# Scheduler ranks for small-tile products, and a reversed operand order in their groups, in a bidirectional RWKV-7 and gated-MLP trunk

## The chip, the cores and the metric

The kernel is one program on one core of a Trainium2 chip. The metric is device time in microseconds (us) of one execution; several executions are made and the median is given. The engines that matter here are PE (TensorE, the matmuls), DVE (VectorE), ACT (ScalarE) and POOL (GpSimd). Each engine works through its own queue of instructions in order and waits on semaphores where an operand comes from another engine or from a DMA.

## The reference

Two residual layers and a final norm over x of 1 x 256 x 2048. Layer 0 is a bidirectional RWKV-7 mixer: one wide projection, token shift, then for 64 heads of width 64 a state recurrence in both directions. Layer 1 is a gated MLP whose spatial mixing takes 128 positions at a time. All that the change touches belongs to layer 0:

```python
def wkv_scan(r, w, k, v, a, b, reverse):
    # S_t = S_(t-1) diag(w_t) + (S_(t-1) a_t) b_t^T + v_t k_t^T ;  y_t = S_t r_t
    ...

def rwkv7_bidir_mixer(h, w_in, mu_prev, mu_next, ...):
    z = h @ w_in
    zs, gate = z[..., :SHIFT_COLS], z[..., SHIFT_COLS:]
    zs = zs + mu_prev * (shift_prev(zs) - zs) + mu_next * (shift_next(zs) - zs)
    r, k, v, dw, da = jnp.split(zs, ...)
    ...
    for d, rev in ((0, False), (1, True)):
        wll = -jax.nn.softplus(-(w0[d] + jnp.tanh(dw[:, :, d]) @ w_up[d])) - 0.5
        decay = jnp.exp(-jnp.exp(wll))
        a_d = jax.nn.sigmoid(a0[d] + da[:, :, d] @ a_up[d])
        k_d = k * (1.0 + (a_d - 1.0) * k_a)
        y = y + wkv_scan(rh, heads(decay), heads(k_d), vh, -kk, kk * heads(a_d), rev)
        bonus = bonus + jnp.sum(rh * heads(k_d) * r_k, axis=-1, keepdims=True) * vh
    yn = (group_norm(y) * ln_w + ln_b)
    return ((yn + bonus) * jax.nn.silu(gate)) @ w_out
```

## The kernel before

Layer 0 is cut into 16 blocks (NB) of 256 of the 4096 branch columns, four heads each. In one block two tiles of 128 columns (`cl` or `l`) hold two heads each, and the two heads of a tile lie in the two halves of the 128 partitions: `h` = 0 is the lower half, `h` = 1 the upper (`H[h]`). The 256 tokens are cut into four chunks of 64 (`c`, or `i` in the recurrence), and there are two directions `d`. The recurrence is done chunk by chunk in matrix form, so a block consists of large products and of many small ones:

- **Full products** are the projections. `mains` computes k, r, v and g of a block (PSUM tiles `acck`, `accr`, `accv`, `accg`). Weights come by DMA as f32 and are split into a high part (`whi`, ACT, L150) and a low part (`wlo`, DVE, L151); `mm3` (L165, L166, L167) then makes three products for each tile of weights: high weights with the high part of the activations, high with low, low with high. Each is 128x128 weights on 128x256 data, and one of k, r, v, g of a block takes 96 of them. `rates` makes the low-rank decay products `up` in the same way.
- **gp** (`grams`, L584): for one direction and one `cl`, four chunks times two halves, eight products. Each contracts over 64 partitions, that is over one half of PE's rows: h=0 the lower half, h=1 the upper. There is one PSUM tile for each half. Both have the tag `pg`, which has two buffers; DVE multiplies each with the mask into `Gs` (L589) and so frees it. `bp` (L606) and other transposed factors use `pg`, too.
- **qp** (`inverses`, L651 and L657): 32x32 products of the triangular inverse. DVE solves the 32x32 diagonal blocks in a loop (L637 to L639) and transposes them (`TD`, L642; `Tn`, L643); L651 takes `Tn`.
- **The recurrence** (`chain`): for each chunk i, eight products of 64 columns in each group. xp (L714, takes the state SUV), yp with RC (L717), then `Xs` copied by ACT, uu (L723), copied back into SUV by ACT (L725), then sp (L730) and yp (L732), DVE makes the next state, and ACT copies it into SUV (L742). Here h picks a half of PE's columns (the output rows); the contraction is over all rows.
- **vp** (L674, transposes of v), **bb** (L769) and **yt** (`finish`, L777, transposes of the normed output, 16 of them) close a block.

The parts of a block are generators that yield a due time within a period; a loop at the end of the layer always advances the one with the smallest due time, and this sets the order of the program text: in one pass it interleaves the projections of block p with grams and inverses of block p-1 and the recurrence of block p-2. This order is not the order of the engines. The kernel is built with

```python
    with _tile.TileContext(nc, schedule_with_timeline_sim=True) as tc:
```

which means that the framework simulates the engines' time lines while it builds and gives each engine, step by step, an instruction whose operands it expects to be ready; among the ready ones it takes the one that stands first in the program text. So small products are placed among the full ones at build time, one by one; a group of eight can be cut.

What the change touches: the loops that issue gp, qp, xp, yp, uu, sp and yt, and the generator `each` that gives the order of (d, l, h) in the recurrence's groups.

Of the kernel before, what the change touches and what calls it, by code (L numbers as in the profile page):

```python
# [22 lines left out]
def trunk(tc, x, norm_g, final_norm_g, w_in, mu_prev, mu_next, w0, w_up, a0, a_up, k_k, k_a, r_k,  # L23
          ln_w, ln_b, w_out, g_w_in, g_ln_g, g_ln_b, g_w_s, g_b_s, g_w_out, out):
    nc = tc.nc
    V, S, G, PE = nc.vector, nc.scalar, nc.gpsimd, nc.tensor
# [9 lines left out]
    C = 64  # L36
    NC = T // C
# [392 lines left out]

    MT = PERIOD / 16
    dt = 4 * MT / KT

# [136 lines left out]
    def grams(b, f, d):  # L572

        AR, BK = f["AR"], f["BK"]
        if d == 0:
            f["Gs"] = sc.tile([P, 2, 16, 2 * C], F32, tag="Gs", name=f"Gs{b}", bufs=2)
        Gs = f["Gs"]
        for cl in range(2):
            yield TGP[d][cl]

            gp = [sm(f"gp{b}_{h}{d}{cl}").rearrange("p (c q t) -> p c q t", c=NC, q=2) for h in range(2)]
            for c in range(NC):
                for h in range(2):
                    PE.matmul(gp[h][:, c].rearrange("p q t -> p (q t)"),  # L584
                              BK[H[h], d, cl, c].rearrange("p q t -> p (q t)"),
                              AR[H[h], d, cl, c].rearrange("p q t -> p (q t)"), start=True, stop=True)
            u0 = (d * 2 + cl) * NC
            for h in range(2):
                V.tensor_tensor(Gs[:, h, u0:u0 + NC], gp[h].rearrange("p c q t -> p c (q t)"),  # L589
                                gmask[:, d].rearrange("p q t -> p (q t)").unsqueeze(1).to_broadcast([P, NC, 2 * C]),  # L590
                                ALU.mult)
# [19 lines left out]
    def inverses(b, f):  # L611

        Gs, AR = f["Gs"], f["AR"]

        def lane(name):
            return se.tile([P, 16 * 33], F32, tag="ln", name=f"{name}{b}", bufs=3)

        Dt = lane("Dt")[:, :512].rearrange("p (t u) -> p t u", u=16)
        NQ = sc.tile([P, 16, 32], F32, tag="vy", name=f"NQ{b}", bufs=2)
        for h in range(2):  # L620
            for q in range(2):
                r0 = h * 64 + q * 32
                S.copy(Dt[r0:r0 + 32].rearrange("p t u -> p u t"), Gs[q * 32:q * 32 + 32, h, :, q * 32:q * 32 + 32])
            nc.sync.dma_start(NQ[h * 64:h * 64 + 32], Gs[0:32, h, :, 32:64])
        yield TSUB[0]
        La = se.tile([P, 32, 32], F32, tag="La", name=f"La{b}")
        V.transpose(La, Dt.unsqueeze(2).to_broadcast([P, 32, 2, 16]))
        xs = lane("X")
        G.memset(xs[:, :512], 0.0)
        G.tensor_scalar(xs.rearrange("p (m r) -> p m r", r=33)[:, :, 0:32:16], diag, 1.0, None, ALU.mult)  # L630
        X = xs[:, :512].rearrange("p (s t) -> p s t", t=16)
        TD = lane("TD")[:, :512]
        for j in range(31, 0, -1):
            yield TSUB[1] - (TSUB[1] - TSUB[0] - 2) * j / 31
            m, n = j // 2, 16 - j // 2
            tv = TD[:, :j * n].rearrange("p (s t) -> p s t", t=n)
            V.tensor_tensor(tv, La[:, j, 0:j].unsqueeze(2).to_broadcast([P, j, n]),  # L637
                            X[:, j:j + 1, m:].to_broadcast([P, j, n]), ALU.mult)
            V.tensor_tensor(X[:, 0:j, m:], X[:, 0:j, m:], tv, ALU.add)  # L639
        yield TSUB[1]  # L640
        Tn = lane("Tn")[:, :512]
        V.transpose(TD.rearrange("p (u t h) -> p t h u", t=16, h=2), X.rearrange("p s t -> p t s"))  # L642
        V.transpose(Tn, TD)  # L643
        TD, Tn = [t.rearrange("p (u t) -> p u t", t=32) for t in (TD, Tn)]
        qp = sm(f"qp{b}", "pq", 1).rearrange("p (u t) -> p u t", t=32)
        R0 = [slice(h * 64, h * 64 + 32) for h in range(2)]
        R1 = [slice(h * 64 + 32, h * 64 + 64) for h in range(2)]
        yield TQ[0]
        for u in range(16):
            for h in range(2):  # L650
                PE.matmul(qp[R1[h], u], NQ[R0[h], u], Tn[R0[h], u], start=True, stop=True)  # L651
        for h in range(2):
            S.copy(NQ[R1[h]], qp[R1[h]])
        yield TQ[1]
        for u in range(16):
            for h in range(2):
                PE.matmul(qp[R0[h], u], NQ[R1[h], u], TD[R1[h], u], start=True, stop=True)  # L657
# [30 lines left out]
    def chain(b, f):  # L688
# [6 lines left out]
        def part(name, i):  # L695
            return sm(f"{name}{b}_{i}", "pc", 1)[:, :256].rearrange("p (n v) -> p n v", v=C)

        def each(i):

            for d, l in DL:  # L700
                for h in range(2):
                    yield d, l, h, (d * 2 + l) * NC + i, SUV[:, d, l, i, h]

        def y(d, l, h, i):
            return yp[H[h], l if d == 0 else 1 - l, i if d == 0 else NC - 1 - i]

        SJ = None
        for i in range(NC):
            t = TCH + CT * i
            yield t  # L710

            xp = part("xp", i)
            for d, l, h, u, suv in each(i):
                PE.matmul(xp[H[h], d * 2 + l], Gs[:, h, u, 0:C], suv, start=True, stop=True)  # L714
            if i > 0:
                for d, l, h, u, suv in each(i):
                    PE.matmul(y(d, l, h, i), RC[:, h, u], suv, start=False, stop=False, skip_group_check=True)  # L717
            Xs = sc.tile([P, 4, C], F32, tag="Xs", name=f"Xs{b}_{i}")
            S.copy(Xs, xp)
            yield t + CB[0]  # L720
            up = part("uu", i)
            for d, l, h, u, _ in each(i):
                PE.matmul(up[H[h], d * 2 + l], TTs[:, h, u], Xs[:, d * 2 + l], start=True, stop=True)  # L723
            for h in range(2):
                S.copy(SUV[H[0], :, :, i, h].rearrange("p d l v -> p (d l) v"), up[H[h]])  # L725
            yield t + CB[1]
            if i < NC - 1:
                sp = part("sp", i)
                for d, l, h, u, suv in each(i):
                    PE.matmul(sp[H[h], d * 2 + l], BT[:, h, u], suv, start=True, stop=True)  # L730
            for d, l, h, u, suv in each(i):
                PE.matmul(y(d, l, h, i), Gs[:, h, u, C:2 * C], suv, start=False, stop=False, skip_group_check=True)  # L732
# [13 lines left out]
    def finish(b, f):  # L746
# [24 lines left out]
        V.tensor_tensor(OT, bb, Vt, ALU.mult)  # L771
        yield TYT
        yt = sm(f"yt{b}", "pc", 1).rearrange("p (l t) -> p l t", l=2)
        for cl in range(2):
            for c in range(NC):
                for h in range(2):
                    PE.matmul(yt[H[h], cl, c * C:(c + 1) * C], yn[:, cl * NC + c], ident[:, H[h]],  # L777
                              start=True, stop=True)
        SG = f["SG"]
        for cl in range(2):  # L780
            j = 2 * b + cl
# [390 lines left out]
```

## Time and profile before

| | before |
|---|---|
| median of 3 runs | 2211.72 us (2210.79 to 2213.2) |
| the profiled execution, whole | 2209.93 us |
| the profiled execution, span | 2208.1 us |
| mean granted TensorE clock | 0.994 |
| layer 0's blocks in the span | about 40 to 1420 us, some 78 us a block |

How to read the rows. "busy" is the time in which an engine worked, x the count of instructions. A timeline row gives start, duration, engine, line, operation, output <- inputs by the program's names (block numbers left out), tile shape, and how many neighbouring records it joins; an f32 product is two records, so x16 is a group of eight products. A matmul's duration is longer than the distance to the next, since PE pipelines them; costs are therefore taken between starts. A row of waits gives the waiting engine, tile and line, what released it, the time, how often, and the longest. In the table of windows, behind the window and its length, stand the busy times of PE, PEld (weight loads), DVE, ACT and POOL with counts, then the granted clock, the DMA share and GB/s. A window of 156 us is two blocks.

### The profile page before, as it was taken

What the parts mean: (1) busy time and instruction counts of PE and PEld (TensorE: products, weight loads), DVE (VectorE), ACT (ScalarE), POOL (GpSimd) and SP (SyncE); (2) the same over time, 40 slices, a digit from 0 to 9 for tenths busy, and PEclk for the clock granted to TensorE, in tenths of its full rate; (3) what the DMA queues carried; (4) which work ended last, traced back from release to release, by engine and by line L of the source; (5) the groups of instructions that cost most, each with busy time, mean ns of one, the idle gap of its engine ahead of it and who ended that gap; (6) DMA issues with size and microseconds to landing.
All of it is one profiled execution on the core that took longest, in us unless ns stands there. A gap on an engine that the chain in (4) does not pass through costs nothing.

```text
span 2208.1 us, 48735 instructions
## 1 busy us (share of the span) xinstructions
PE 2169.0 (98%) x19984; PEld 1938.5 (88%) x19984; DVE 1611.7 (73%) x3121; ACT 1289.0 (58%) x2032; POOL 160.7 (7%) x230
## 2 busy tenths in 40 slices
PE   7999999999999999999999999999999999999998
PEld 7899999999999999999999877788888888888886
DVE  5788788888887988897888764475456777777444
ACT  6556666757666766766676654464444444444443
POOL 2210110111101100010011000000000000000000
PEclk9899999999999999999999999999999999999999
DMA  5556455454555555555555565676766666666664
GB/s 167 141 144 158 116 130 135 131 138 128 139 134 146 140 137 137 143 139 139 145 140 135 167 193 179 195 248 191 229 200 191 193 196 193 195 197 191 196 195 153
DMA packets 403374, 362.30 MB, mean 164 GB/s; under 512 B 128848, under 2 KB 350800, under 8 KB 403024
## 3 DMA queue, kind: packets, MB, share of 16 engines
q1 hardware_dynamic: 382896, 337.96, 53.9%
q10 hardware_dynamic: 20256, 21.24, 3.0%
q8 instruction: 157, 2.57, 0.5%
q14 instruction: 65, 0.53, 0.1%
HBM read 329.78 MB, written 6.29 MB: 152 GB/s over the span
## 4 chain that ended last, share of the span: by engine, by line
PE 77%; DMA 8%; DVE 7%; ACT 6%; issue 2%; POOL 0%; SPq 0%; ACTq 0%; POOLq 0%; DVEq 0%
PE uacc L204 5%; PE gacc L204 5%; DMA raw_o<-in_rwkv_w_out_dram 3%; PE gp L584 3%; PE oacc L166 3%; PE oacc L167 3%; PE oacc L165 3%; PE uacc L206 3%; PE gacc L206 3%; PE vacc L165 3%; PE vacc L166 3%; PE vacc L167 3%; PE accg L167 2%; PE accv L167 2%; PE accv L165 2%; PE accv L166 2%
## 5 line engine op out<-in xcount | busy, mean ns | idle before, releaser
L204 PE MATMUL uacc<-z,whi_u 128*128 128x512 f32 x512 | 179.0, 394 | 0.0
L204 PE MATMUL gacc<-z,whi_g 128*128 128x512 f32 x512 | 177.3, 393 | 0.0
L165 PE MATMUL acck<-zh,whi_wk 128*128 128x256 f32 x512 | 151.1, 295 | 1.6 <-ACT whi_wk L150 1.6
L167 PE MATMUL accg<-zh,wlo_wg 128*128 128x256 f32 x512 | 149.2, 291 | 3.1 <-DVE wlo_wg L151 2.8
L165 PE MATMUL accg<-zh,whi_wg 128*128 128x256 f32 x512 | 151.9, 297 | 0.0
L167 PE MATMUL accr<-zh,wlo_wr 128*128 128x256 f32 x512 | 149.3, 292 | 0.1
L165 PE MATMUL accv<-zh,whi_wv 128*128 128x256 f32 x512 | 148.9, 291 | 0.0
L165 PE MATMUL accr<-zh,whi_wr 128*128 128x256 f32 x512 | 148.9, 291 | 0.0
L166 PE MATMUL accr<-zl,whi_wr 128*128 128x256 f32 x512 | 148.8, 291 | 0.0
L167 PE MATMUL accv<-zh,wlo_wv 128*128 128x256 f32 x512 | 148.4, 290 | 0.1
L167 PE MATMUL acck<-zh,wlo_wk 128*128 128x256 f32 x512 | 146.1, 285 | 1.0 <-DVE wlo_wk L151 1.0
L166 PE MATMUL accv<-zl,whi_wv 128*128 128x256 f32 x512 | 146.7, 287 | 0.0
L166 PE MATMUL acck<-zl,whi_wk 128*128 128x256 f32 x512 | 146.0, 285 | 0.0
L166 PE MATMUL accg<-zl,whi_wg 128*128 128x256 f32 x512 | 145.7, 285 | 0.0
L206 PE MATMUL uacc<-z,wlo_u 128*128 128x256 f32 x512 | 142.4, 284 | 0.0
L206 PE MATMUL gacc<-z,wlo_g 128*128 128x256 f32 x512 | 140.2, 279 | 0.0
L151 DVE TENSOR_TENSOR wlo_v<-raw_v,whi_v 128x1024 fp32r<-128x1024 f32 x64 | 78.4, 1225 | 80.4 <-ACT whi_v L150 80.4
L639 DVE TENSOR_TENSOR X<-X,TD 128x126 f32<-128x126 f32 (+22 forms) x496 | 127.1, 256 | 10.7
L637 DVE TENSOR_TENSOR TD<-La,X 128x126 f32<-128x126 f32 (+22 forms) x496 | 125.0, 252 | 10.8
L151 DVE TENSOR_TENSOR wlo_o<-raw_o,whi_o 128x1024 fp32r<-128x1024 f32 x64 | 78.2, 1224 | 72.4 <-ACT whi_o L150 72.1
L151 DVE TENSOR_TENSOR wlo_p<-raw_p,whi_p 128x1024 fp32r<-128x1024 f32 x60 | 73.9, 1232 | 75.7 <-ACT whi_p L150 75.7
L150 ACT CAST whi_p<-raw_p 128x1024 fp32r<-128x1024 f32 x60 | 63.1, 1051 | 91.5 <-PE oacc L167 87.3
(328 smaller groups left out, 6750.7 us busy)
## 6 DMA issues: line engine op xcount, KB each, us to landing
raw_wk<-in_rwkv_w_in_dram SPq DMA_DIRECT2D x64, 512.0 KB, 3.7
raw_wr<-in_rwkv_w_in_dram SPq DMA_DIRECT2D x64, 512.0 KB, 3.9
raw_wv<-in_rwkv_w_in_dram SPq DMA_DIRECT2D x64, 512.0 KB, 3.7
raw_wg<-in_rwkv_w_in_dram SPq DMA_DIRECT2D x64, 512.0 KB, 3.8
raw_o<-in_rwkv_w_out_dram SPq DMA_DIRECT2D x64, 512.0 KB, 3.9
raw_v<-in_gmlp_w_in_dram SPq DMA_DIRECT2D x64, 512.0 KB, 4.2
raw_u<-in_gmlp_w_in_dram SPq DMA_DIRECT2D x64, 512.0 KB, 3.5
raw_g<-in_gmlp_w_in_dram SPq DMA_DIRECT2D x64, 512.0 KB, 3.6
```

What stands on the lines that cost most here:

```text
L150: latest[0] = S.copy(hi, raw)
L151: latest[1] = V.tensor_tensor(lo, raw, hi.bitcast(F32), ALU.subtract)
L165: PE.matmul(acc, a[0], b[0], start=first, stop=False, skip_group_check=True)
L166: PE.matmul(acc, a[0], b[1], start=False, stop=False, skip_group_check=True)
L167: PE.matmul(acc, a[1], b[0], start=False, stop=last, skip_group_check=True)
L204: PE.matmul(acc.rearrange("p h t -> p (h t)"), hi[:, j, cs], zc[:, k].rearrange("p h t -> p (h t)"), start=k == 0, stop=False, skip_group_ ...
L206: PE.matmul(acc[:, 0], lo[:, j, cs], zc[:, k, 0], start=False, stop=k == KT - 1, skip_group_check=True)
L584: PE.matmul(gp[h][:, c].rearrange("p q t -> p (q t)"), BK[H[h], d, cl, c].rearrange("p q t -> p (q t)"), AR[H[h], d, cl, c].rearrange("p q ...
L637: V.tensor_tensor(tv, La[:, j, 0:j].unsqueeze(2).to_broadcast([P, j, n]), X[:, j:j + 1, m:].to_broadcast([P, j, n]), ALU.mult)
L639: V.tensor_tensor(X[:, 0:j, m:], X[:, 0:j, m:], tv, ALU.add)
```

## The change

`small_tiles(rank)` opens a context in which every instruction gets a priority that is higher by rank x 100000 than its place in the text gives it. gp gets rank 1, yt 2, qp 3 and the recurrence's products 4. The projections, bp, vp, bb, the rate products and the work of all other engines stay as they are. In addition the order within groups is turned: gp and `each` take h=1 before h=0, and yt takes the second `cl` and the last chunk first. No instruction is added or taken away on any engine.

```diff
+    def small_tiles(rank=1):
+        return tc.high_priority(offset=rank * 100000)
...
-            for c in range(NC):
-                for h in range(2):
-                    PE.matmul(gp[h][:, c].rearrange("p q t -> p (q t)"),
+            with small_tiles():
+                for c in range(NC):
+                    for h in (1, 0):
+                        PE.matmul(gp[h][:, c].rearrange("p q t -> p (q t)"),
...
-        for u in range(16):
-            for h in range(2):
-                PE.matmul(qp[R1[h], u], NQ[R0[h], u], Tn[R0[h], u], start=True, stop=True)
+        with small_tiles(3):
+            for u in range(16):
+                for h in range(2):
+                    PE.matmul(qp[R1[h], u], NQ[R0[h], u], Tn[R0[h], u], start=True, stop=True)
...
         def each(i):
             for d, l in DL:
-                for h in range(2):
+                for h in (1, 0):
                     yield d, l, h, (d * 2 + l) * NC + i, SUV[:, d, l, i, h]
...
-            for d, l, h, u, suv in each(i):
-                PE.matmul(xp[H[h], d * 2 + l], Gs[:, h, u, 0:C], suv, start=True, stop=True)
-            if i > 0:
+            with small_tiles(4):
                 for d, l, h, u, suv in each(i):
-                    PE.matmul(y(d, l, h, i), RC[:, h, u], suv, start=False, stop=False, skip_group_check=True)
+                    PE.matmul(xp[H[h], d * 2 + l], Gs[:, h, u, 0:C], suv, start=True, stop=True)
+                if i > 0:
+                    for d, l, h, u, suv in each(i):
+                        PE.matmul(y(d, l, h, i), RC[:, h, u], suv, start=False, stop=False, skip_group_check=True)
...
-        for cl in range(2):
-            for c in range(NC):
-                for h in range(2):
-                    PE.matmul(yt[H[h], cl, c * C:(c + 1) * C], yn[:, cl * NC + c], ident[:, H[h]],
+        with small_tiles(2):
+            for cl in (1, 0):
+                for c in reversed(range(NC)):
+                    for h in range(2):
+                        PE.matmul(yt[H[h], cl, c * C:(c + 1) * C], yn[:, cl * NC + c], ident[:, H[h]],
```

The second qp group (L657 before) is ranked 3 like the first, and uu (L723), sp (L730) and yp (L732) are ranked 4 like xp. Line numbers of the kernel after are 6 to 12 higher.

How the engines' queues differ is shown at three places. In the names, the number behind the letters is the block, what stands behind the underscore comes from the builder; xN joins equal neighbours.

**First place: a product of yp beside its group.** PE's queue while the full products of r of block 10 (`accr10`) run; `sp8_1` and `yp8` belong to chunk 1 of block 8's recurrence. Before:

```order
L167 MATMUL accr10_10903<-zh_187,wlo_wr10_4_10829 128x256
L165 MATMUL accr10_10903<-zh_187,whi_wr10_4_10828 128x256
L732 MATMUL yp8_10663<-SUV8_10606,Gs8_9324 64x64
L166 MATMUL accr10_10903<-zl_188,whi_wr10_4_10828 128x256
L730 MATMUL sp8_1_10943<-SUV8_10606,BT8_10046 64x64 x8
L732 MATMUL yp8_10663<-SUV8_10606,Gs8_9324 64x64 x7
L167 MATMUL accr10_10903<-zh_187,wlo_wr10_4_10829 128x256
```

and of the change:

```order
L167 MATMUL accr10_10903<-zh_187,wlo_wr10_8_10907 128x256
L406 MATMUL hs_k10_11040<-bones_85,SQ10_10924 128x2 x3
L741 MATMUL sp8_1_10943<-SUV8_10606,BT8_10046 64x64 x8
L743 MATMUL yp8_10663<-SUV8_10606,Gs8_9324 64x64 x8
L406 MATMUL hs_k10_11040<-bones_85,SQ10_10924 128x2
L165 MATMUL accr10_10903<-zh_187,whi_wr10_8_10906 128x256
```

The one yp product that stood ahead of a full product is back with its seven fellows; `hs_k10` (128x2 products of `factors`) now stands on both sides of the group.

**Second place: the halves of gp.** PE's queue, gp of block 10, direction 1; in `gp10_010` the three digits behind the underscore are h, d and cl, so `gp10_010` is the lower half and `gp10_110` the upper, both of cl=0. Before, among products of k of block 11:

```order
L167 MATMUL acck11_11746<-zh_187,wlo_wk11_0_11666 128x256
L714 MATMUL xp9_0_11775<-SUV9_11710,Gs9_10428 64x64 x8
L584 MATMUL gp10_010_11786<-AR10_11176,BK10_11389 128x128
L584 MATMUL gp10_110_11787<-AR10_11176,BK10_11389 128x128
L584 MATMUL gp10_010_11786<-AR10_11176,BK10_11389 128x128
L584 MATMUL gp10_110_11787<-AR10_11176,BK10_11389 128x128
L584 MATMUL gp10_010_11786<-AR10_11176,BK10_11389 128x128
L584 MATMUL gp10_110_11787<-AR10_11176,BK10_11389 128x128
L584 MATMUL gp10_010_11786<-AR10_11176,BK10_11389 128x128
L584 MATMUL gp10_110_11787<-AR10_11176,BK10_11389 128x128
L165 MATMUL acck11_11746<-zh_187,whi_wk11_0_11665 128x256
```

Of the change, among products of g of block 9, the same eight products, and then the eight of cl=1:

```order
L166 MATMUL accg9_11476<-zl_188,whi_wg9_8_11479 128x256
L590 MATMUL gp10_110_11787<-AR10_11176,BK10_11389 128x128 x4
L590 MATMUL gp10_010_11786<-AR10_11176,BK10_11389 128x128 x4
L682 MATMUL vp9_11712<-ident_78,Vt9_11469 128x128 x2
L167 MATMUL accg9_11476<-zh_187,wlo_wg9_8_11480 128x256
```

```order
L167 MATMUL accg9_11476<-zh_187,wlo_wg9_8_11480 128x256
L590 MATMUL gp10_111_11834<-AR10_11176,BK10_11389 128x128 x4
L165 MATMUL accg9_11476<-zh_187,whi_wg9_8_11479 128x256
L166 MATMUL accg9_11476<-zl_188,whi_wg9_8_11479 128x256
L167 MATMUL accg9_11476<-zh_187,wlo_wg9_8_11480 128x256
L165 MATMUL accg9_11476<-zh_187,whi_wg9_8_11479 128x256
L590 MATMUL gp10_011_11833<-AR10_11176,BK10_11389 128x128 x4
L166 MATMUL accg9_11476<-zl_188,whi_wg9_8_11479 128x256
```

Before, the halves alternate. Now four products of the upper half come first, then four of the lower: for cl=0 next to each other, for cl=1 with four full products between them. All stand some 180 rows further ahead in the queue.

**Third place: the first products of qp and the transposes that make their operand.** DVE's queue around the transpose into `Tn9`, block 9. Before:

```order
L151 TENSOR_TENSOR wlo_wg9_4_11396<-raw_wg9_4_11393,whi_wg9_4_11395 128x1024
L643 STREAM_TRANSPOSE Tn9_11293<-TD9_10766 128x512
L756 BN_AGGR mv8_11407<-st6_8_11406 128x2 x2
L396 SCALAR_TENSOR_TENSOR Vt9_11469<-accv9_11179,pc_114,Vt9_11469 128x255
L771 TENSOR_TENSOR OT8_11467<-bb8_11465,Vt8_10365 128x512
```

and of the change:

```order
L645 TENSOR_TENSOR X9_10763<-X9_10763,TD9_10766 128x16
L648 STREAM_TRANSPOSE TD9_10766<-X9_10763 128x32x16
L396 SCALAR_TENSOR_TENSOR rt10_11159<-accr10_10903,pc_114,rt10_11159 128x255
L649 STREAM_TRANSPOSE Tn9_11293<-TD9_10766 128x512
L750 TENSOR_TENSOR SJ8_2_11137<-sp8_2_11120,SJ8_1_10960 128x256
L398 SCALAR_TENSOR_TENSOR rt10_11159<-accr10_10903,pc_114,rt10_11159 128x255
```

PE's queue at the first products of qp in the same block, before (among products of g of block 9):

```order
L165 MATMUL accg9_11476<-zh_187,whi_wg9_0_11335 128x256
L166 MATMUL accg9_11476<-zl_188,whi_wg9_0_11335 128x256
L651 MATMUL qp9_11296<-Tn9_11293,NQ9_10742 32x32 x32
L167 MATMUL accg9_11476<-zh_187,wlo_wg9_0_11336 128x256
L165 MATMUL accg9_11476<-zh_187,whi_wg9_4_11395 128x256
```

and of the change (among products of v of block 9 and the rate products of block 10):

```order
L165 MATMUL accv9_11179<-zh_187,whi_wv9_4_11168 128x256
L166 MATMUL accv9_11179<-zl_188,whi_wv9_4_11168 128x256
L658 MATMUL qp9_11296<-Tn9_11293,NQ9_10742 32x32 x32
L612 MATMUL bp9_10_11215<-ident_78,BK9_10285 128x128 x4
L612 MATMUL bp9_11_11229<-ident_78,BK9_10285 128x128 x4
L167 MATMUL accv9_11179<-zh_187,wlo_wv9_4_11169 128x256
```

Behind L649 in the second excerpt stand the line numbers of the kernel after (L643 before). Both moved ahead, qp from the end of the first tile of weights of g to the second tile of v, and the transpose to a place among the token shifts of r of block 10.

More of the change, by code (lines that the diff above doesn't have):

```diff
@@ L581, in grams @@
             gp = [sm(f"gp{b}_{h}{d}{cl}").rearrange("p (c q t) -> p c q t", c=NC, q=2) for h in range(2)]
-            for c in range(NC):
-                for h in range(2):
-                    PE.matmul(gp[h][:, c].rearrange("p q t -> p (q t)"),
-                              BK[H[h], d, cl, c].rearrange("p q t -> p (q t)"),
-                              AR[H[h], d, cl, c].rearrange("p q t -> p (q t)"), start=True, stop=True)
+            with small_tiles():
+                for c in range(NC):
+                    for h in (1, 0):
+                        PE.matmul(gp[h][:, c].rearrange("p q t -> p (q t)"),
+                                  BK[H[h], d, cl, c].rearrange("p q t -> p (q t)"),
+                                  AR[H[h], d, cl, c].rearrange("p q t -> p (q t)"), start=True, stop=True)
             u0 = (d * 2 + cl) * NC
@@ L654, in inverses @@
         yield TQ[1]
-        for u in range(16):
-            for h in range(2):
-                PE.matmul(qp[R0[h], u], NQ[R1[h], u], TD[R1[h], u], start=True, stop=True)
+        with small_tiles(3):
+            for u in range(16):
+                for h in range(2):
+                    PE.matmul(qp[R0[h], u], NQ[R1[h], u], TD[R1[h], u], start=True, stop=True)
         for h in range(2):
@@ L721, in chain @@
             up = part("uu", i)
-            for d, l, h, u, _ in each(i):
-                PE.matmul(up[H[h], d * 2 + l], TTs[:, h, u], Xs[:, d * 2 + l], start=True, stop=True)
+            with small_tiles(4):
+                for d, l, h, u, _ in each(i):
+                    PE.matmul(up[H[h], d * 2 + l], TTs[:, h, u], Xs[:, d * 2 + l], start=True, stop=True)
             for h in range(2):
@@ L726, in chain @@
             yield t + CB[1]
-            if i < NC - 1:
-                sp = part("sp", i)
+            with small_tiles(4):
+                if i < NC - 1:
+                    sp = part("sp", i)
+                    for d, l, h, u, suv in each(i):
+                        PE.matmul(sp[H[h], d * 2 + l], BT[:, h, u], suv, start=True, stop=True)
                 for d, l, h, u, suv in each(i):
-                    PE.matmul(sp[H[h], d * 2 + l], BT[:, h, u], suv, start=True, stop=True)
-            for d, l, h, u, suv in each(i):
-                PE.matmul(y(d, l, h, i), Gs[:, h, u, C:2 * C], suv, start=False, stop=False, skip_group_check=True)
+                    PE.matmul(y(d, l, h, i), Gs[:, h, u, C:2 * C], suv, start=False, stop=False, skip_group_check=True)
             if i < NC - 1:
@@ L773, in finish @@
         yt = sm(f"yt{b}", "pc", 1).rearrange("p (l t) -> p l t", l=2)
-        for cl in range(2):
-            for c in range(NC):
-                for h in range(2):
-                    PE.matmul(yt[H[h], cl, c * C:(c + 1) * C], yn[:, cl * NC + c], ident[:, H[h]],
-                              start=True, stop=True)
+        with small_tiles(2):
+            for cl in (1, 0):
+                for c in reversed(range(NC)):
+                    for h in range(2):
+                        PE.matmul(yt[H[h], cl, c * C:(c + 1) * C], yn[:, cl * NC + c], ident[:, H[h]],
+                                  start=True, stop=True)
         SG = f["SG"]
```

## The prediction

> **What bounds the kernel now.** The page comes first: engine totals and the clock.
>
> ```profile
> span 2208.1 us, 48735 instructions
> ...
> PE 2169.0 (98%) x19984; PEld 1938.5 (88%) x19984; DVE 1611.7 (73%) x3121; ACT 1289.0 (58%) x2032; POOL 160.7 (7%) x230
> ...
> PEclk9899999999999999999999999999999999999999
> ```
>
> PE is busy for 98% of the span, at full granted clock after the start. A busy PE need not be an efficient one, so I next ask whether it waits inside the stage that the change touches (the recurrent layer, about 40 to 1420 us), by the table of windows.
>
> ```profile
> 198.00:354.00 156.00, 154.16 (x1985) 142.59 (x1985) 126.89 (x300) 102.68 (x182) 13.62 (x20) 1.00 0.50 131
> ...
> 666.00:822.00 156.00, 156.00 (x1977) 145.93 (x1976) 130.09 (x305) 107.21 (x188) 13.79 (x20) 1.00 0.53 140
> ```
>
> After the length come the busy times of PE, its weight loads, DVE, ACT and POOL. PE has 1.8 us of idle time in 156 us early on and none at all from 666 to 822 us. So in this stage PE's queue itself is the time: whatever shortens or lengthens the sequence of matmuls arrives nearly whole at the end. The list of PE's waits says how much of it small products lose to late operands:
>
> ```profile
> PE yp L732 <- ACT SUV L725: 1.4, 2, 0.8
> PE xp L714 <- ACT SUV L681: 1.3, 1, 1.3
> ...
> PE qp L657 <- ACT NQ L653: 0.9, 1, 0.9
> ...
> PE uu L723 <- DMA Gs<-AR: 0.5, 1, 0.5
> ```
>
> These four rows make 4.1 us in the whole run. That is all that "operand not there yet" can give back; the rest has to come from how the matmuls stand in PE's queue.
>
> **What a small product costs by where it stands.** The timeline of PE shows starts and durations. One f32 product is two records. First a **visit**: the stream of full products, cut by one group of small ones:
>
> ```profile
> 727.05 0.28 PE L165 MATMUL accr<-zh,whi_wr 128*128 128x256 f32 x1
> 727.26 0.69 PE L723 MATMUL uu<-Xs,TTs 128*64 128x64 f32 x16
> 727.88 0.39 PE L166 MATMUL accr<-zl,whi_wr 128*128 128x256 f32 x1
> 728.10 0.28 PE L167 MATMUL accr<-zh,wlo_wr 128*128 128x256 f32 x1
> ```
>
> Full products follow each other at 0.12 us (three more rows below show it). Entering takes 0.21 instead of 0.12 (+0.09), and the second full product behind the group comes 0.22 instead of 0.12 after the first (+0.10). Now two kinds of small product in one visit, and two groups of one kind:
>
> ```profile
> 701.49 0.69 PE L723 MATMUL uu<-Xs,TTs 128*64 128x64 f32 x16
> 702.11 1.16 PE L584 MATMUL gp<-AR,BK 64*128 64x128 f32 x16
> 703.20 0.39 PE L165 MATMUL acck<-zh,whi_wk 128*128 128x256 f32 x1
> 703.42 0.28 PE L166 MATMUL acck<-zl,whi_wk 128*128 128x256 f32 x1
> 703.54 0.28 PE L167 MATMUL acck<-zh,wlo_wk 128*128 128x256 f32 x1
> ...
> 705.54 0.69 PE L730 MATMUL sp<-SUV,BT 128*64 128x64 f32 x16
> 706.05 0.64 PE L732 MATMUL yp<-SUV,Gs 128*64 128x64 f32 x16
> 706.62 0.39 PE L165 MATMUL acck<-zh,whi_wk 128*128 128x256 f32 x1
> ```
>
> From uu to gp, another tile shape, it takes 0.62 us, as from uu to a full product; from sp to yp, the same shape, 0.51. So leaving a shape costs about 0.1 us, whatever follows. I call an unbroken run of one shape a stay: **a stay costs 0.1 us, and a visit to small products from full ones 0.19 us on top.**
>
> A lone product of yp, cut off from its group by one full product:
>
> ```profile
> 717.07 0.28 PE L165 MATMUL accr<-zh,whi_wr 128*128 128x256 f32 x1
> 717.27 0.33 PE L732 MATMUL yp<-SUV,Gs 128*64 128x64 f32 x2
> 717.53 0.38 PE L166 MATMUL accr<-zl,whi_wr 128*128 128x256 f32 x1
> 717.85 0.69 PE L730 MATMUL sp<-SUV,BT 128*64 128x64 f32 x16
> 718.36 0.64 PE L732 MATMUL yp<-SUV,Gs 128*64 128x64 f32 x14
> 718.93 0.39 PE L167 MATMUL accr<-zh,wlo_wr 128*128 128x256 f32 x1
> ```
>
> From 717.07 to the start of sp pass 0.78 us. Without the lone product it would be 0.12 + 0.21 = 0.33, and yp's last part takes 0.57 us with 14 records as with 16. So **a lone product costs 0.45 us.**
>
> Last, the products gp, which use one half of PE's rows each: h=0 the lower, h=1 the upper. The order of these four groups, by the program's order, is: alternating halves; four of one half and nothing else; four, then four of the other; three, three, then one and one.
>
> ```profile
> 599.43 1.16 PE L584 MATMUL gp<-AR,BK 64*128 64x128 f32 x16
> 600.53 0.39 PE L165 MATMUL accg<-zh,whi_wg 128*128 128x256 f32 x1
> ...
> 440.99 1.16 PE L584 MATMUL gp<-AR,BK 64*128 64x128 f32 x8
> 442.07 0.39 PE L165 MATMUL accg<-zh,whi_wg 128*128 128x256 f32 x1
> ...
> 246.57 1.71 PE L584 MATMUL gp<-AR,BK 64*128 64x128 f32 x16
> 248.21 0.39 PE L165 MATMUL accv<-zh,whi_wv 128*128 128x256 f32 x1
> ...
> 455.09 1.49 PE L584 MATMUL gp<-AR,BK 64*128 64x128 f32 x16
> 456.50 0.38 PE L165 MATMUL accg<-zh,whi_wg 128*128 128x256 f32 x1
> ```
>
> Eight products in alternation take 1.10 us, four of one half alone 1.08: two products of different halves run side by side, two of one half don't. Four and four take 1.64, three-three-one-one 1.41.
>
> **The change, part by part.** No product is added or taken away, so only counts of places change. I counted them in the two orders of PE.
>
> 1. Lone products of yp: 21 before, none now. 21 x 0.45 = **-9.5 us**. This is the first place quoted above.
> 2. Other stays: 382 - 21 = 361 before, 333 now. -28 x 0.1 = **-2.8 us**.
> 3. Other visits: 296 - 21 = 275 before, 289 now. The ranked groups go when they are ready instead of next to each other. +14 x 0.19 = **+2.7 us**.
> 4. gp's halves, 64 groups of eight. Before: 31 alternate, 6 stand three-three-one-one, 1 four-four, and 26 are broken up, mostly in alternation. Now: 23 alternate, 11 are three-three-one-one or near it, 14 four-four in one stay, 12 four and four in two visits, 4 broken otherwise. Over an alternating group, three-three-one-one costs 1.41 - 1.10 = 0.31, four-four 0.54, and two stays 2 x 1.08 - 1.10 = 1.06, less 0.1 for the stay that is counted already: 0.96. A broken group in alternation is bounded by 0 (nothing lost) and 0.96 (all of one half); nearest is three-three-one-one, so 0.31. Before 6 x 0.31 + 0.54 + 26 x 0.31 = 10.5; now 11 x 0.31 + 14 x 0.54 + 12 x 0.96 + 4 x 0.31 = 23.7. **+13.2 us**. With the broken ones at 0.1 it would be +16.5, at 0.5 +9.1.
> 5. The reversed order of h and of yt's chunks changes no product's own cost: halves or column tiles swap places. It only makes the group start on the operand that is made last. I cost it at 0; the bounds are -4.1 us (the four waits above vanish) and rival 2.
>
> The sum is -9.5 - 2.8 + 2.7 + 13.2 = **+3.6 us**. The profiled execution took 2209.93 us (span 2208.1 and 1.8 around it), so it would be 2213.5; the median of the three runs is 2211.72, 1.8 higher, and there it gives **2215.3 us**. What hides it: nothing, since PE is never idle in the middle of the stage. Only what lies before about 200 us, where PE waits for weights anyway, is covered; one to two of the 16 blocks lie there, and the orders differ little in them.
>
> [...] On weight loads, the view of the tile uu from 900 to 980 us says:
>
> ```profile
> L723 PEld LDWEIGHTS uu<-Xs,TTs x64: 132/138/138, 928.7 to 969.7; 128*64 128x64 f32 x64
> ```
>
> [...]
>
> **Rivals.**
>
> *1, faster: the halves of gp cost nothing on the way, or the waits go.* If what follows a one-half group filled its free rows, item 4 would fall away: 2215.3 - 13.2 = 2202. Against it, after four of one half the next full product comes at 1.08, not earlier. If instead the four waits go and the broken groups were dearer than I take them (+9.1), it is 2215.3 - 4.1 - 4.1 = 2207.
>
> *2, slower: the first qp products become a wait for DVE.* In blocks 9 to 15, qp's first half moves up PE's queue (third place in the order, with DVE's transposes). Before, its operand was ready well ahead:
>
> ```profile
> 904.71 0.71 DVE L643 STREAM_TRANSPOSE Tn<-TD 128x512 f32<-128x512 f32 x1
> ...
> 907.73 0.66 PE L651 MATMUL qp<-Tn,NQ 32*32 32x32 f32 x30
> ```
>
> That is 907.73 - 905.42 = 2.3 us. From block 10's first product of r to qp, PE's queue now holds 17.8 us less work at the prices above (of it 99 full products, 11.9 us), and DVE's queue from wlo_wr10_0 to the transposes 15.9 us less, at the mean durations of its lines. So 0.4 us of the 2.3 are left. If DVE loses more than that on the way, each microsecond is paid in seven blocks: +7 us, and full products queue behind the waiting one. From about 0.15 us a block on, with the forecast, it is slower by over 0.2%; at 1 us it is 2222, and if DVE did not follow at all, 15.5 x 7 = 108 us. Against it, 0.4 is still positive, and DVE is idle for 26 us in 156, so it can make up ground.
>
> *3, the change does not do what it says:* the groups are not joined, because the count of visits falls by 7 of 296 only. It is in the sum: joining yp and parting gp from its neighbours nearly cancel. A rank that joins everything would have given items 1 and 2 alone, 2199; the order excludes it.
>
> **Chances.** The forecast (2212 to 2218, waits about as before) 0.52; rival 1 with gp free 0.10, with the waits gone 0.18; rival 2 0.20. Rival 3's 2199 has none. A difference of 0.2%, 4.4 us, is about what a measurement of this kernel can tell from none, so "same" is 2207.3 to 2216.1. The forecast gives 0.36 there and 0.16 above it; rival 1 with gp free is faster, with the waits gone 0.07 faster and 0.11 same; rival 2 is slower. Faster 0.17, same 0.47, slower 0.36. The range runs from 2205 (between rival 1's two times) to 2225 (rival 2 with 1.4 us a block), which leaves out some 0.1 below and 0.1 above. The likeliest case's own range is 2212 to 2218.
>
> **What would show it.** In the timeline after, no yp row of x2 stands alone; sp x16 and yp x16 follow each other. gp rows of x16 last about 1.7 us where they go four and four, and rows of x8 1.16 us in two visits; the busy time of gp in the table of groups, now
>
> ```profile
> L584 PE MATMUL gp<-AR,BK 64*128 64x128 f32 x1024 | 96.4, 292 | 2.3 <-DVE Gs L589 1.7 <-POOL BK L556 0.5
> ```
>
> rises from 96.4 us by about the 13.2 us of item 4. PE stays at 156.0 of 156 in the middle blocks, and the length of such a block changes by little. Waits of qp at L658 on DVE's transposes would show rival 2, waits of xp and yp that are gone rival 1. The prediction is wrong if the early blocks (200 to 560 us), where most lone products are joined, do not shorten, or if new waits of more than a few tenths come up in each of the later blocks.

## The result, and the profile after

| | before | change |
|---|---|---|
| median, first series | 2211.64 us (4 runs, 2210.79 to 2213.2) | 2225.32 us (4 runs, 2223.68 to 2226.83) |
| ratio | | 1.0061, 95% interval 1.0043 to 1.0078 |
| the profiled execution, whole and span | 2209.93 and 2208.1 us | 2223.96 and 2222.2 us |
| ratio in a second series, beside the experiments | | 1.0047, 1.0029 to 1.0064 (2204.12 and 2213.45 us) |

The change is slower by 13.7 us in the first series, 0.3 us beyond the upper end of the range, and by 9.3 us in the second (medians; 10.4 by the ratio). The windows of the changed kernel in the middle of the recurrent layer, columns as before:

```profile
198.00:354.00 156.00, 154.85 (x1992) 144.82 (x1990) 127.35 (x298) 103.68 (x182) 13.88 (x20) 1.00 0.51 132
666.00:822.00 156.00, 153.58 (x2065) 144.13 (x2063) 131.00 (x307) 105.27 (x185) 15.46 (x20) 1.00 0.54 138
822.00:978.00 156.00, 153.69 (x1906) 143.99 (x1904) 128.32 (x300) 103.02 (x179) 15.11 (x20) 1.00 0.52 136
```

PE was busy for 156.00 of 156 us from 666 to 822 us, and in the next window too:

```profile
822.00:978.00 156.00, 156.00 (x1957) 146.34 (x1957) 133.02 (x316) 107.55 (x184) 13.11 (x21) 1.00 0.54 140
```

Now 2.4 us are idle in the one and 2.3 us in the other. The prediction said that this number stays. The list of PE's waits (waiting tile, releaser; total, times, longest) names what is late:

```profile
PE uu L733 <- ACT Xs L728: 4.5, 5, 1.8
PE xp L723 <- ACT SUV L753: 3.7, 7, 1.0
PE hs_k L406 <- ACT SQ L497: 3.3, 2, 2.6
PE sp L741 <- ACT SUV L735: 2.7, 4, 0.9
```

These are 14.2 us for four rows. Before, the same list has 2.6 us for uu, xp, hs_k and sp together: beside the rows of uu (0.5) and xp (1.3) that the prediction quoted, these two.

```profile
PE xp L714 <- ACT SUV L742: 0.4, 1, 0.4
PE hs_k L406 <- ACT SQ L492: 0.4, 1, 0.4
```

The four rows that the prediction quoted came to 4.1. All four releasers in the list of the change are ACT; behind which work ACT came late differs, and is told at e11. No row of qp waiting for DVE is in this list.

Where the time went along the span can be read from one instruction of each block, the activation of the gate behind g's last product (start, duration, engine, line). Before:

```profile
544.73 0.60 ACT L450 ACTIVATE SG<-accg 128x512 f32<-128x512 f32 x1
...
1231.27 0.60 ACT L450 ACTIVATE SG<-accg 128x512 f32<-128x512 f32 x1
```

and the same two blocks after:

```profile
523.36 0.59 ACT L455 ACTIVATE SG<-accg 128x512 f32<-128x512 f32 x1
...
1245.94 0.60 ACT L455 ACTIVATE SG<-accg 128x512 f32<-128x512 f32 x1
```

At the first of these marks the change is 21 us ahead, at the second, nine blocks later, 15 us behind. But the first is the extreme one of the stage: PE's queue of the change still has small products to do at it that the kernel before has done (128 records of qp, 34 of gp and 32 of yt, among others). One block later the same activation stands at

```profile
617.47 0.60 ACT L450 ACTIVATE SG<-accg 128x512 f32<-128x512 f32 x1
...
612.58 0.60 ACT L455 ACTIVATE SG<-accg 128x512 f32<-128x512 f32 x1
```

before and after, and the gain is 4.9 us. (Some 9 us of the early gain are the granted clock: the kernel before lost 10.4 us by it between 60 and 160 us, the changed one 1.8, as the windows of 20 us add up.) So the marks show a gain first and a loss later; how large each is depends on the mark.

gp's row in the table of groups, for the fourth term of the sum:

```profile
L590 PE MATMUL gp<-AR,BK 64*128 64x128 f32 x1024 | 103.5, 288 | 2.9 <-DVE Gs L595 1.9 <-POOL BK L561 0.8
```

It rose from 96.4 to 103.5 us, by 7.1 and not by 13.2.

A last reading divides the whole difference. For each matmul record I took the time to the next record's start, without the idle time that the profile shows in front of that next one, and summed it by tile; idle time is summed apart. Differences to the kernel before, in us, of one profiled execution each (a lower clock is contained in all but the waits):

| | full products | yp | yt, xp, sp | gp | others | PE's waits | total |
|---|---|---|---|---|---|---|---|
| change, first series | -1.3 | -5.7 | -5.5 | +8.3 | -0.1 | **+18.4** | +14.1 |
| change, second series | -5.4 | -6.0 | -6.5 | +7.1 | +0.2 | **+7.8** | -2.8 |

The places of the products, everything but the waits, give -4.3 us, or about -1 when the clock's share (13.6 us lost before, 10.2 after) is taken out. The prediction had +3.6. What it lacked is the column of waits. The second row is the same program; its execution was the fastest of four (2207.05 us), and it is set against the kernel before of the first series. It lost some 8.5 us less by the clock than that one, so its places are worth about -2 us and the waits +7.8. The wait of hs_k and some of the weights' waits are not in it; that of uu is, and those of xp and sp in part. The size of the waits thus differs by 10 us between two executions of one program; their sign doesn't.

### The profile page after: what moved, and what is told of

It reads as the page before. It is cut to its first block, busy times and chain, and to the rows that moved or that the text cites. A ratio compares the mean times of both kernels' runs of the same rounds, so it can differ in the third digit from the quotient of the medians.

```text
span 2222.2 us, 48767 instructions
## 1 busy us (share of the span) xinstructions
PE 2164.9 (97%) x19984; PEld 1938.3 (87%) x19984; DVE 1611.1 (72%) x3121; ACT 1287.1 (58%) x2032; POOL 172.7 (8%) x230
## 4 chain that ended last, share of the span: by engine, by line
PE 56%; DVE 16%; DMA 13%; ACT 10%; issue 3%; POOL 1%; ACTq 0%; SPq 0%; POOLq 0%; DVEq 0%
PE uacc L204 5%; PE gacc L204 5%; DMA raw_o<-in_rwkv_w_out_dram 3%; PE oacc L166 3%; PE oacc L167 3%; PE oacc L165 3%; PE uacc L206 3%; PE gacc L206 3%; DMA raw_wk<-in_rwkv_w_in_dram 3%; PE vacc L165 3%; PE vacc L166 3%; PE vacc L167 3%; DMA raw_wr<-in_rwkv_w_in_dram 2%; DVE wlo_wg L151 2%; PE accr L167 2%
## 5 line engine op out<-in xcount | busy, mean ns | idle before, releaser
L643 DVE TENSOR_TENSOR TD<-La,X 128x126 f32<-128x126 f32 (+22 forms) x496 | 124.8, 252 | 11.0
```

## The experiments

All ran beside the kernel before, which took 2204 to 2205 us in that series; ratios are to it, and 0.1% is 2.2 us; the us are worked out from the ratio. "Places by count" in the expectations is a sum from the order of PE's queue alone, at prices from the trace of before. The last two columns divide one profiled execution of each kernel as in the table above, against the one before, with the time that the lower clock costs taken out: what the places of the products give, and what PE's waits give.

| kernel | ranks | reversed | ratio (95%) | us | places by count | places | waits |
|---|---|---|---|---|---|---|---|
| e1 | none | all | 0.9974 (0.9958 to 0.9989) | -5.7 | -4 | -13 | 0 |
| e5 | none | recurrence, gp | **0.9940** (0.9917 to 0.9962) | -13 | -7.4 | -16 | +2 |
| e10 | yt | all | **0.9937** (0.9918 to 0.9955) | -14 | -5.6 | -15 | 0 |
| e8 | recurrence | all | 0.9966 (0.9951 to 0.9981) | -7.5 | -1.4 | -8 | +3 |
| e9 | qp | all | 1.0031 (1.0013 to 1.0049) | +6.8 | -2.2 | -11 | +12 |
| e4 | gp | all | 1.0065 (1.0040 to 1.0090) | +14 | +8.6 | +6 | +6 |
| e2 | all but gp | all | 1.0002 (0.9993 to 1.0012) | +0.4 | -3.7 | -9 | +8 |
| e13 | all but qp | all | 1.0002 (0.9989 to 1.0016) | +0.4 | +4.2 | -4 | +1 |
| e3 | all but the recurrence | all | 1.0076 (1.0053 to 1.0099) | +17 | +3.6 | -4 | +12 |
| e7 | all | none | 1.0098 (1.0075 to 1.0120) | +22 | +6.4 | +12 | +6 |
| e12 | all (the change) | all | 1.0047 (1.0029 to 1.0064) | +10 | +2.7 | -2 | +8 |
| e6 | none, gp by halves | none | 1.0103 (1.0078 to 1.0128) | +23 | +16 | +29 | -9 |
| e11 | all, Dt on POOL | all | 0.9987 (0.9975 to 0.9999) | -2.9 | -5.0 | -15 | +5 |

In the first trace of the change the two are about 0 and +18. The places come out 3 to 10 us better than by count in eleven of the thirteen; e6 and e7, which reverse nothing, come out 13 and 6 us worse.

### e1 to e4: order and ranks apart

e1 takes every rank away from the change and keeps the reversed orders; e2, e3 take one rank away; e4 leaves gp's alone. Each edit is of this kind (here e2):

```diff
-            with small_tiles():
+            with nullcontext():
                 for c in range(NC):
                     for h in (1, 0):
                         PE.matmul(gp[h][:, c].rearrange("p q t -> p (q t)"),
```

> The three reversed orders (gp, the recurrence's groups, yt) without any rank. Two theories of the changed kernel's +13.7 us (2225.3 against 2211.6): PLACES gives it to where the small products stand in PE's queue, WAITS-CHAIN gives some 11 us of it to waits that the recurrence's rank makes (PE reaches a ranked group before ACT has copied its operand), WAITS-GP gives those 11 us to the rank of gp, which moves gp's masks, ACT's copies of the result and a DMA behind them. Counted in the order, the places alone are worth about -4 us here (no lone yp product is left, 284 visits instead of 296, and gp keeps mostly alternating). No rank, so no new waits: both WAITS theories expect about 2207.5 us. If places are dearer than counted, or waits come from the reversed order, it is 2212 or more.

> The change without gp's rank (reversed orders and the ranks of yt, qp and the recurrence kept). Places by count: -3.7 us against the kernel before, 6.4 us less than the change. WAITS-CHAIN: the 11 us of waits stay, 2211.6 - 3.7 + 11 = about 2219 us. WAITS-GP: they go, about 2208 us.

> The change without the recurrence's rank (reversed orders and the ranks of gp, yt and qp kept). Places by count: +3.6 us. WAITS-CHAIN: the waits of uu, sp and xp on ACT go, about 2215 us. WAITS-GP: they stay, about 2226 us.

> Reversed orders and gp's rank alone. Places by count: +8.6 us (226 neighbours of one half in gp against 72 before, 387 stays). WAITS-CHAIN: about 2220 us. WAITS-GP: 11 more, about 2231 us.

Without any rank the kernel is 5.7 us faster than before, so the reversed orders are no loss, they are the gain. (e1's ten runs spread from 2191.9 to 2206.0 us, more than others', so its size is less sure than its sign.) Without gp's rank the loss is gone; without the recurrence's rank it stays (1.0076, whose interval overlaps with that of the change). Of the two theories of the waits, the one that puts them down to the recurrence's own rank expected 2219 and 2215 us for e2 and e3 and is wrong on both. The theory that puts them down to gp's rank is right on e3 and on the sign of e2; e4, at 1.0065, falls between the two (1.0038 and 1.0088 by their sums). But it can't be all: e2 still lies 6 us above e1, and this row is in its list of waits:

```profile
PE uu L733 <- ACT Xs L728: 5.6, 6, 1.7
```

Nor are waits the main thing that gp's rank adds. The waits of e2 (+8 us) are as many as those of the change's second trace (+8), while its places are 7 us better (-9 against -2), and this is gp's own time: +1.1 us against before in e2, +8.5 in both traces of the change. So gp's rank costs mainly by its halves, which is the fourth term of the prediction. And the recurrence's rank has a part in uu's waits, since their row falls to 1.1 us in e3.

### e5, e7: which part joins the products

```diff
-        with small_tiles(2):
+        with nullcontext():
-            for cl in (1, 0):
-                for c in reversed(range(NC)):
+            for cl in range(2):
+                for c in range(NC):
...
```

is e5, with all other ranks taken away as in e1. e7 is the change with the three old orders.

> No rank, and only the order of h turned, in the recurrence's groups and in gp (yt as before). The first experiment fell by 5.7 us with all three reversals. JOINED BY ORDER: the reversal alone puts yp's lone products back into their groups, because ACT makes the operand's half h=1 last, so that nothing of the group is ready before all of it is; by count no lone product is left, 270 visits, places -7.4 us: about 0.997 of before. JOINED BY RANK (the prediction's wording): without a rank it brings little, 0.999 to 1.001.

> All four ranks with the old orders. JOINED BY ORDER: the lone products of yp stay (38 by count, against 24 before and none in the change), places +6.4 us, and the waits of the ranks come on top, some 8 us: ratio about 1.006 to 1.007. JOINED BY RANK: like the change or better, 1.006 or less with no lone yp row in the trace.

e5 is 13 us faster than before, with no rank at all. e7, with all ranks, is the slowest but one (1.0098 where 1.006 to 1.007 was expected), and its timeline still shows a lone product of yp (x2) in front of its group:

```profile
870.66 0.33 PE L743 MATMUL yp<-SUV,Gs 128*64 128x64 f32 x2
...
871.23 0.69 PE L741 MATMUL sp<-SUV,BT 128*64 128x64 f32 x16
871.75 0.64 PE L743 MATMUL yp<-SUV,Gs 128*64 128x64 f32 x14
```

(The expectation's count finds 24 lone products before where the prediction's found 21; at 0.45 us each the three are 1.4 us.) So the groups are joined by the order of h, not by the rank. The reading of why: ACT writes SUV in two copies, h=0 first (L725), and in the built orders (of before, the change, e5 and e7) the products into one PSUM tile always stand in the order of the program text. With h=0 first in the text, the first product's operand is ready one copy (0.37 us) ahead of the others', and it is sent off alone. With h=1 first, nothing of the group can go before the last copy, and then all goes. gp's two halves are two PSUM tiles, so nothing holds their order, and a rank lets each go when its buffer is free.

### e6: the price of gp's halves by itself

```diff
-            for c in range(NC):
-                for h in range(2):
+            for h in range(2):
+                for c in range(NC):
                     PE.matmul(gp[h][:, c].rearrange("p q t -> p (q t)"),
```

in the kernel before, with nothing else changed.

> The kernel before with gp's two loops exchanged: all four products of one half, then all four of the other, no rank and no reversal. This measures the fourth item of the prediction by itself: 64 groups at 0.54 us are 34.6 us instead of 10.5, so +24 us by the prediction's prices; prices from the sequences of rows give +16 us. If the halves cost nothing on the way: within 2 us of before.

+22.7 us (17 to 28) by the ratio, and the group's row:

```profile
L584 PE MATMUL gp<-AR,BK 64*128 64x128 f32 x1024 | 128.5, 292 | 1.2 <-DVE Gs L589 1.2
```

The 28 groups that stand unbroken take 1.64 us each, as the prediction's row of four and four does; the other 36 are cut into two or three parts and take 1.88 and 2.15 us on average. gp's own places grow by 30 us, more than the 24 expected, and PE's waits shrink by 9 (a longer group leaves the other engines more time, by my reading). That the sum comes near +24 is therefore in part luck. The halves do cost on the way, and the price is rather too low than too high.

### e8, e9, e10, e13: which rank makes PE wait

Each of the first three is e1 with one rank put back; e13 is the change without qp's.

> All reversals and the rank of the recurrence alone (gp, yt, qp without). By count the places are worth -1.4 us against before. Without gp's rank the change was at 1.0002 and without any rank at 0.9974, so the ranks of yt, qp and the recurrence cost about 6 us together. If the recurrence's rank makes the waits of uu on ACT's copy Xs (5.4 us there): ratio about 1.001 to 1.002, with those waits in the trace. If yt's or qp's rank makes them: about 0.998 to 0.999, without.

> All reversals and the rank of qp alone. Places by count -2.2 us against before (2 us more than with no rank). The recurrence's rank alone was at 0.9966, and with yt's and qp's ranks it was 1.0002. If qp's rank brings the waits of uu on ACT's copy Xs (it lets the recurrence of a block start while ACT still makes the next block's copies Dt): ratio 1.000 to 1.002, with uu waits of 4 us or more. If it is yt's rank: 0.997 to 0.998, without them.

> All reversals and the rank of yt alone. Places by count -5.6 us. If yt's rank makes uu wait: ratio about 1.000. If qp's rank does, or only both together: about 0.997, no uu waits.

> The change without qp's rank (reversals and the ranks of gp, yt and the recurrence kept). qp's rank alone took the reversed kernel from 0.9974 to 1.0031. Places by count +4.2 us against before, 1.5 more than the change. If qp's rank adds its cost beside gp's: about 1.001 to 1.002, with uu's waits on Xs mostly gone. If gp's rank makes the same waits by itself: 1.005 to 1.007.

The recurrence's rank (0.9966) leaves the gain where it is, yt's (0.9937) lies even 8 us below e1, and uu has hardly a wait in either (none in e8's list, 0.8 us in e10's). qp's rank turns -0.26% into +0.31%, with this row:

```profile
PE uu L733 <- ACT Xs L728: 2.8, 4, 1.1
```

That is short of the 4 us or more expected, but all waits of PE together are 12 us more than in e1, about the whole difference of the two: besides uu, gp waits 2.9 us more for its masks, xp some 3.6, hs_k, yt and hb_k some 3 together.

Beside the other ranks qp's costs about the same: 1.0002 without it (e13), 1.0047 with it (e12), 10 us. Here too it is the waits: +1 us in e13, +8 and +18 in the two traces of the change. uu's row gets smaller but does not vanish:

```profile
PE uu L733 <- ACT Xs L728: 1.9, 2, 1.7
```

gp's rank costs 10 us as well, 1.0002 (e2) against 1.0047. Alone they cost some 13 (qp) and 20 us (gp) on top of e1. The expectation that they either add or make the same waits is answered by neither pure case: taking either one out is worth 10 us, which is less than each costs alone. One reason can be read: with gp's rank and without qp's (e4, e13) the products of qp stand in 73 and 74 unbroken runs instead of 34, and their own time grows by 5 us.

### e11: the copies that stand ahead of Xs

What does ACT do while uu waits? The changed kernel's timeline, first ACT, then PE, at the longest such wait:

```profile
547.55 2.13 ACT L629 COPY Dt<-Gs 32x512 f32<-32x512 f32 x2
549.70 0.37 ACT L728 COPY Xs<-xp 128x256 f32<-128x256 f32 x1
...
550.12 0.75 PE L733 MATMUL uu<-Xs,TTs 128*64 128x64 f32 x16 [1.79 <-ACT Xs L728]
```

ACT makes the four copies Dt (1.07 us each) of the next block's inverse in a row, and Xs, 0.37 us, comes behind them. PE's next instruction is uu, and 1.8 us pass. On average Xs starts 0.64 us behind xp's end before the change, 1.37 us in it, 1.32 in e2, 1.16 in e9, and 0.60 in e5. The waits of sp late in the stage have another cause:

```profile
860.00 1.05 ACT L150 CAST whi_wr<-raw_wr 128x1024 fp32r<-128x1024 f32 x1 [1.08 <-DMA raw_wr<-in_rwkv_w_in_dram]
860.96 0.74 ACT L735 COPY SUV<-uu 64x256 f32<-64x256 f32 x2
...
861.75 0.45 PE L741 MATMUL sp<-SUV,BT 128*64 128x64 f32 x8 [0.61 <-ACT SUV L735]
```

Here ACT stands for 1.08 us before a cast of weights that are still arriving, the cast takes 1.05, and the copy that PE needs is queued behind both. The long wait of hs_k (2.56 us) is of the same kind: ACT stood for 4.07 us before a cast of weights, and made SQ behind it. The waits of xp on SUV are not a queue of ACT at all. In each of the seven, ACT is idle for 1.6 to 2.5 us in front of that copy, until DVE has made the next state:

```profile
1023.02 0.82 ACT L753 COPY SUV<-SJ 64x256 f32<-64x256 f32 x2 [1.83 <-DVE SJ L748]
...
1023.89 0.69 PE L723 MATMUL xp<-SUV,Gs 128*64 128x64 f32 x16 [0.76 <-ACT SUV L753]
```

In this one, DVE made the low part of a tile of weights first, which had waited for ACT's cast and so for the weights. e11 takes Dt away from ACT:

```diff
-                S.copy(Dt[r0:r0 + 32].rearrange("p t u -> p u t"), Gs[...])
+                G.tensor_copy(Dt[r0:r0 + 32].rearrange("p t u -> p u t"), Gs[...])
```

> The change, with the four copies Dt of each block on POOL instead of ACT; nothing else is edited, but the built order moves with it (places by count -5.0 us against before, 7.7 less than the change, mostly fewer neighbours of one half in gp: 152 instead of 212). If the waits of uu on Xs come from Dt standing ahead of Xs in ACT's queue, uu's 4 us go, and with the places it is some 12 us below the change: about 1.001. If ACT only lags in general, or the waits come from weights that arrive late, uu still waits and only the places help: about 1.003.

The ratio went to 0.9987, 13 us below e12, and uu's waits to

```profile
PE uu L733 <- ACT Xs L728: 0.2, 1, 0.2
```

So the 4 us of uu are gone, as expected if Dt makes them. The rest is places, and they moved by more than the 8 us expected (-15 against -2 in e12), so the built order changed with the edit and e11 does not show Dt alone. gp now waits more for its masks (6.5 us in three waits, by the list), and the ten executions had a mean granted clock of 0.990 to 0.994, those of the kernel before beside them 0.994 to 0.998; both count against this version.

### e12: the change again

> The changed kernel itself, unedited, beside the other runs of this study and on their chip: 1.006, as at first (1.0061), if the chips agree.

1.0047, whose interval overlaps with that of 1.0061. In its trace uu waits as before it,

```profile
PE uu L733 <- ACT Xs L728: 4.6, 5, 1.8
```

but hs_k's wait of 2.6 us has shrunk to 0.3, so most of it, a late transfer of weights, belongs to the execution and not to the order.

## Why the prediction was wrong

**The bound** was right in the main: the sequence on PE is the time. But what is added there arrives only less what it takes from the waits (e6: 30 us of places, 9 us of waits gone).

**Item 1, lone products (-9.5 us)**: the size is borne out as far as it can be read, the cause was wrong. They are gone, sp x16 and yp x16 follow each other, and yp's own time fell by 5.7 us, which fits 24 lone products at the 0.26 us of the row at 717.27. The rest of the price lies, by the same rows, at the full products around them, where other visits change too. But item 5 priced the reversed order at 0 "since it changes no product's own cost", while it is the reversal that joins the groups. e5 has it without ranks: -13 us (-18 to -8), against -9.5 - 1.4 (stays) - 1.0 (visits) by the prediction's prices, and gp 4 us better than before. e1, which reverses yt's order too, has it with -5.7 us (-9 to -2).

**Items 2 and 3** (-2.8, +2.7) nearly cancel in the sum; they were not tried one by one. What is left of the gain beside item 1 stands at yt, xp and sp, -5.5 us, 4 of it at yt, whose groups are cut less often.

**Item 4, gp's halves (+13.2 us)**: the prices of unbroken groups hold, that of the broken ones was mis-sized. gp's time rose by 8.3 us in one trace of the change and by 7.1 in the other (8.5 in both without the clock). The 26 broken groups of the kernel before were taken at 0.31 us each over an alternating group, the price of three-three-one-one. In its trace 17 of them, in two parts, take 1.60 us on average and 9, in three parts, 1.85: 0.59 us over the 1.10, so the kernel before was already 7.3 us dearer here than the sum had it. The prediction's other figure, 0.5 us each and +9.1 in all, is the nearer one. (Its figure for 0.1 us, +16.5, should be +17.9 by its own counts.)

**Item 5 and the forecast's "waits about as before": this is the step that failed.** The prediction looked at four waits that might vanish (4.1 us; the same list has 4.7 us more of small products, 2.2 of it at gp) and at one that might come, qp for DVE. Waits grew by 18.4 us in one trace and by 7.8 in the other. 11.6 of the 18.4 stand at uu, xp, sp and hs_k (14.2 against 2.6). For uu, sp and hs_k a copy or activation of ACT of 0.4 to 0.5 us is queued behind copies, or behind casts of weights, of 1 us; for xp it is DVE's state that comes late. The prediction's own second sign of being wrong, new waits in the later blocks, came true. The reading is this: a rank moves an instruction of PE to the front as soon as its operand is expected; it doesn't move what the operand's engine does in front of it. Before, the full products that stood ahead of such a group covered that delay. Had waits stayed as they were, the change would have been near no difference, with the places at about -1.

**Rival 2** had the right sign and half of the culprit: qp's rank costs 10 us, in waits. Its mechanism was wrong. qp did not wait for DVE's transposes in either trace of the change (in e3 it did, for 1.1 us). With the earlier qp, uu falls where ACT makes the next Dt (e9, e11). gp's rank costs its 10 us mainly by the halves (e2 against the change). Whether it makes waits too stays open: the first trace of the change has 10 us more of them than e2, the second none. **Rival 1** needed free halves, or waits that go with broken groups that are dearer; only the dearer broken groups came. **Rival 3** ("the groups are not joined") missed that they are joined by another part of the change.

The clock was left out of the sum. It differs between the two profiled executions of the first series by 3.4 us in favour of the change and hides that much of the loss between these two.

## What to carry to other kernels

Where PE is always busy and a scheduler places its instructions, a rank on PE's products alone can turn the cover of their operands into waits (here qp's did, +12 us of waits in e9; the recurrence's and yt's alone hardly, +3 in e8 and 0 in e10); ask for each ranked group which engine makes its operand, and what stands ahead of that in the engine's queue. A group into one PSUM tile that begins with the operand made last stays together without any rank: here the versions with the reversal and neither gp's nor qp's rank are at 0.994 to 0.997 of the time (e5, e10, e8, e1), and e5 is the simplest of the two best. Price the places and the waits apart, each from its own rows, since a new order changes both and they need not go the same way.

## What the runs showed of the hardware

In the trace of the change one wait of PE cost twice. Towards the end of the 2.6 us wait of hs_k (557.3 to 559.9 us)

```profile
559.89 1.01 PE L406 MATMUL hs_k<-bones,SQ 128*128 128x2 f32 x4 [2.56 <-ACT SQ L497]
```

the granted clock (the number before the last two) fell to a half for about 7 us:

```profile
556.00:558.00 2.00, 1.33 (x11) 1.12 (x10) 0.51 (x3) 0.00 (x0) 0.00 (x0) 1.00 0.82 241
558.00:560.00 2.00, 0.10 (x1) 0.11 (x1) 0.53 (x1) 1.46 (x2) 0.00 (x0) 0.81 0.07 23
560.00:562.00 2.00, 2.00 (x10) 2.00 (x11) 1.90 (x7) 0.81 (x2) 0.00 (x0) 0.50 0.13 7
...
564.00:566.00 2.00, 2.00 (x28) 1.78 (x29) 1.93 (x4) 0.65 (x2) 0.00 (x0) 0.50 0.01 4
566.00:568.00 2.00, 2.00 (x28) 1.93 (x25) 0.57 (x2) 0.22 (x1) 0.00 (x0) 0.98 0.69 201
```

From 558 to 566 us that is 0.4 + 3 x 1.0 = 3.4 us of lost clock, some 0.3 of it in the wait itself, so about 3 us more. Full products start 0.21 us apart there (562.41, 562.62 and 562.84 us, for instance), against 0.12 before the wait (556.58, 556.69 and 556.81). The second trace of the same program (e12), where that wait is missing, keeps the clock over the same stretch:

```profile
556.00:572.00 16.00, 16.00 (x194) 15.27 (x194) 15.59 (x41) 11.29 (x24) 0.76 (x2) 1.00 0.34 101
```

By finer windows of the same trace, the granted clock was 1.00 up to 559.25 us, 1.9 us into the wait, 0.51 in the quarter of a us behind that, 0.50 up to 566.0 and 1.00 again from 566.1 us on.

How long a wait was does not tell here whether it cost clock. uu's wait of 1.79 us, from 548.33 us on in the trace of the change, cost none: the clock was 1.00 in every window from 546 to 552 us. A wait of yt of 0.60 us, which ended at 616.93 us in the same trace, was followed from about 617.3 to 620.7 us by a clock of 0.50, while PE was busy all the time. And in e2, where PE was idle for 1.74 of the 20 us from 540 to 560, the mean clock of this stretch was 0.91. What decides it was not shown.
